# Weight-stationary products in a fused three-block kernel: the two passes of each k-tile one behind the other, instead of eight of the one kind and then eight of the other

## The chip, the cores and the metric

The kernel runs on one core of a Trainium2 chip. The metric is the device time of one execution in microseconds (us); several executions are timed and the median is given. One further execution is recorded instruction by instruction, and every duration below comes from that record. TensorE does the matrix products, VectorE and ScalarE the elementwise work; GpSimd does next to nothing here, and SyncE issues the transfers of the weights.

## The reference

Three transformer blocks run one after the other over 256 tokens of width 1024, all in float32. Blocks 0 and 1 are alike and have their own weights; block 2 has another mixer. What is computed, cut to its shape:

```python
# blocks 0 and 1
h = rms_norm(x, g_pre_mix)
q, k, v, cb, cc, cx, ga, gb = split(h @ w_in)          # 1024 x 6656
y_attn = band_attention(rope(q), rope(k), v, sink) @ w_attn_proj
y_conv = (cb * short_conv(cc * cx, conv_w)) @ w_conv_proj
x = x + rms_norm((sigmoid(ga) * y_attn + sigmoid(gb) * y_conv) @ w_out, g_post_mix)
h = rms_norm(x, g_pre_ffn)
x = x + rms_norm((silu(h @ w_gate) * (h @ w_up)) @ w_down, g_post_ffn)   # inner width 2816
# block 2: a condition vector c gives shifts, scales and gates (silu(c) @ w_cond + b_cond);
# its mixer is a stick-breaking attention beside a trailing mean; its feed-forward part is as above
```

All weights are read from HBM once per execution.

## The kernel before

**Two-part products.** TensorE takes a reduced float32 form here (`F32R`). To keep the accuracy, the kernel splits an operand into a high part H, a copy rounded to that form, and a low part L, the rest. A product of an activation x and a weight w is made of three parts, xH·wH, xL·wH and xH·wL; the fourth is left out. ScalarE writes H of the weights (line 278), VectorE writes L (line 280).

**The weight stream.** The weights are packed in pieces of 128 x 2048 in the order of use (`ORDER`). SyncE loads each as two halves of 128 x 1024 into seven buffers (`emit_raw`, line 258); `emit_half` splits each half into H and L, with twelve buffers for each of them. `get(key)` hands out the next piece, and sees to it that pieces some places further on are loaded and split.

**Two kinds of products.** In the token-major kind (`mmA4`, `mmD2`) the activations are the stationary operand and 512 columns of weights stream past them; each k-tile costs two matmuls of 512 columns with wH and one of 512 with wL. In the weight-stationary kind, `mmB` (line 439), a 128 x 128 tile of weights is loaded into the array and the activations of all 256 tokens stream past. The pair (xH, xL) lies side by side (`xp.hl(k)`), so that one matmul of 512 columns does xH·wH and xL·wH, into the two halves of one PSUM tile `o`; a matmul of 256 columns adds xH·wL to the first half (`xp.k(0, k)` is xH). For one output block of 128 columns there are eight k-tiles. `mmB` does two such blocks (`for c in range(2)`), each made of eight matmuls of 512 columns with H, then eight of 256 with L, and `use(c, o)` then adds the two halves of `o` on ScalarE and VectorE (`both`, lines 456 to 458). In what follows, these sixteen matmuls are called a group, and the matmuls the H pass and the L pass of a k-tile. Every matmul has a weight load of its own in front of it.

`mmB` is used for `cc`, `cx`, `cb` of blocks 0 and 1 (line 882 onwards; PSUM tiles `pcc`, `pcx`, `pcb`), and for nine of the pieces of gate and up in each of the three feed-forward parts (lines 568 and 572; tiles `pg`, `pu`). Block 2's mixer does not use it.

**The order around it.** The program order on TensorE is fixed while the kernel is built. A virtual clock (`clock`, advanced by `pe(ns)` after each matmul with a nominal duration) says when waiting tasks are due: a generator handed to `spawn` runs up to its next `yield`, and names there the delay after which it goes on. `tick()` runs whatever is due, so a task's matmuls land only where a `tick()` stands. In `mmB` it stands behind the fourth H pass, behind the eighth, and at the end of the group. The tasks that land in `mmB` are the attention of blocks 0 and 1 (`keys` and eight `unit`s, lines 614 to 706, spaced by `UNIT` = 10 virtual us; a unit transposes q, computes scores `S`, waits `SM_DELAY` = 8 virtual us for the softmax on VectorE and ScalarE, transposes the probabilities into `PTp`, and multiplies by v), and the transposes `ptf` of the feed-forward part (line 541).

Of the kernel before, what the change touches and what calls it, by code (L numbers as in the profile page):

```python
# [21 lines left out]
KT = D // P  # L22
# [140 lines left out]
def tile_model(ctx: ExitStack, tc: tile.TileContext, x_in, wpack, sink, convw, gains, c_in,  # L163
# [15 lines left out]
    def ps1(name, shape=(P, 512), dt=F32):  # L179
        return pp.tile(list(shape), dt, tag="B", name=name, bufs=8)  # L180
# [41 lines left out]
    def pe(ns):  # L222
        clock[0] += ns / 1000.0

    def tick(limit=None):
        limit = clock[0] if limit is None else limit
        while True:
            due = [e for e in tasks if e[0] <= limit]
            if not due:
                return  # L230
            e = min(due, key=lambda v: v[0])
            tasks.remove(e)
            d = next(e[1], None)
            if d is not None:
                tasks.append([max(e[0], clock[0]) + d, e[1]])
# [10 lines left out]
    def mm(o, a, b, start, stop, **kw):  # L246
        nc.tensor.matmul(o, a, b, start=start, stop=stop, **kw)  # L247
# [191 lines left out]
    def mmB(name, w, xp, use):  # L439

        for c in range(2):
            o = ps1(f"{name}_{c}", (P, 2, T))
            H, L = (v.rearrange("p (k c) -> p k c", k=KT) for v in w[c])
            for k in range(KT):
                mm(o, H[:, k, :], xp.hl(k), k == 0, False)
                pe(213)
                if k == 3:
                    tick()
            tick()
            for k in range(KT):  # L450
                mm(o[:, 0], L[:, k, :], xp.k(0, k), False, k == KT - 1)
                pe(107)
            use(c, o)
            tick()

# [78 lines left out]
    def ffn(l, xp, norms, make_post, after, early=lambda: None):  # L534
# [29 lines left out]
        for key in order:  # L564
            cond_due()
            if key[0] == "g":
                s = s2(f"s{l}{key[2]}", (P, 2, T))
                mmB(f"pg{l}{key[2]}", get(key), xp, lambda c, o: both(s[:, c], o))
                last = nc.scalar.activation(s, s, AF.Silu)  # L569
            elif key[0] == "u":  # L570
                fv = s2(f"f{l}{key[2]}", (P, 2, T))
                mmB(f"pu{l}{key[2]}", get(key), xp, lambda c, o: both(fv[:, c], o))
                nc.vector.tensor_mul(fv, fv, s)  # L573
                fHL = s4(f"fHL{l}{key[2]}", (P, 2, 2, T), F32R)
                nc.scalar.copy(fHL[:, 0], fv)  # L575
                nc.vector.tensor_sub(fHL[:, 1], fv, fHL[:, 0].bitcast(F32))
                fs.append((fHL[:, 0], fHL[:, 1]))
            else:
                j = key[2]
                if not accs:  # L580
                    drain()
                    accs = [[ps1(f"dn{l}_{t}{c}") for c in range(2)] for t in range(2)]
                if j == NDOWN - TAIL - 2:
                    early()
                if j < NDOWN - TAIL:
                    w = get(key)
                    for t in range(2):
                        for c in range(2):
                            mmD2(accs[t], w, fs[j][0], fs[j][1], t, c, j == 0, False)
                else:  # L590
                    cap = 2 * (state["use"] - len(tail)) + NSPLIT
                    tail.append((get(key, cap), fs[j][0], fs[j][1]))
# [260 lines left out]
    def mixer1(l, xp, norms):  # L853
# [28 lines left out]
        for j in range(4):  # L882
            cc = s2(f"cc{l}{j}", (P, 2, T))
            mmB(f"pcc{l}{j}", get(("cc", l, j)), xp, lambda c, o: both(cc[:, c], o))
            u = ac.tile([P, 2, T + 2], F32, tag="u", name=f"u{l}{j}", bufs=1)
            nc.vector.memset(u[:, :, 0:1], 0.0)
            nc.vector.memset(u[:, :, T + 1:T + 2], 0.0)
            mmB(f"pcx{l}{j}", get(("cx", l, j)), xp, lambda c, o: both(u[:, c, 1:T + 1], o))
            nc.vector.tensor_mul(u[:, :, 1:T + 1], u[:, :, 1:T + 1], cc)
            y = s2(f"yc{l}{j}", (P, 2, T))  # L890
            for c in range(2):
                w = cw[:, l, 2 * j + c, :]
                nc.vector.tensor_scalar(y[:, c], u[:, c, 0:T], w[:, 0:1], None, ALU.mult)
                nc.vector.scalar_tensor_tensor(y[:, c], u[:, c, 1:T + 1], w[:, 1:2], y[:, c], ALU.mult, ALU.add)
                nc.vector.scalar_tensor_tensor(y[:, c], u[:, c, 2:T + 2], w[:, 2:3], y[:, c], ALU.mult, ALU.add)
            b = s2(f"cb{l}{j}", (P, 2, T))
            mmB(f"pcb{l}{j}", get(("cb", l, j)), xp, lambda c, o: both(b[:, c], o))
            nc.vector.tensor_mul(y, b, y)
            yp.put(2 * j, 2, y)
# [161 lines left out]
    xp = Pair("x0")  # L1061
    norms = None

    for l in range(DEPTH):
        mp = mixer1(l, xp, norms)
        gpm, gpf = row(4 * l + 1, f"gpm{l}"), row(4 * l + 2, f"gpf{l}")
        xp = Pair(f"xf{l}")
# [38 lines left out]
        xp, norms = nxp, nn  # L1106
# [23 lines left out]
    xp = Pair("xf2")  # L1130
# [95 lines left out]
```

## Time and profile before

| | |
|---|---|
| times of three executions | 1142.68, 1144.66, 1146.54 us |
| their median | 1144.66 us |
| the profiled execution: its own time | 1144.54 us |
| its span, first to last instruction | 1142.4 us |
| VectorE busy | 800.3 us (70%) |
| ScalarE busy | 687.2 us (60%) |
| transfers of weights | 422, of 512 KB, median 5.1 us from issue to landing |
| HBM read | 233.28 MB |
| mean granted TensorE clock | 0.998 |

How to read it: a matmul's busy time in such a record runs from its start to its modelled end, and consecutive matmuls overlap, so the busy time of TensorE says that it had something in flight, not what a matmul costs. What a matmul costs in a row of them is the distance between the starts of two neighbours, called a step below.

### The profile page before, as it was taken

The page shows a single profiled execution, that of the slowest core. Times are in us where ns is not written, and L with a number is a line of the kernel's source. Part 1 is how long each engine was busy: PE and PEld are TensorE (multiplying, and loading weights), DVE is VectorE, ACT ScalarE, POOL GpSimd, SP SyncE. Part 2 cuts the span into 40 slices and gives each one's busy share as a digit, 9 for nine tenths or more (in the row PEclk, how much of TensorE's full clock was granted, in tenths as well). Part 3 has the DMA queues.
Part 4 walks back from the last instruction along what each step waited for, and adds up shares of the span by engine and source line. Part 5 has one row for each costly group of instructions (what it writes and reads, how often), then busy time and mean ns, then how long its engine had stood idle before and what let it go on. Part 6 is the DMA issues. An engine that isn't in the chain of part 4 may idle for free.

```text
span 1142.4 us, 15967 instructions
## 1 busy us (share of the span) xinstructions
PE 1132.2 (99%) x5901; PEld 951.7 (83%) x5901; DVE 800.3 (70%) x1188; ACT 687.2 (60%) x1209; POOL 13.4 (1%) x28
## 2 busy tenths in 40 slices
PE   8999999999999999999999999999999999999997
PEld 5888878888888888888878888888888778888886
DVE  7888745658977657798874758977657748866652
ACT  6778766547555446688765556545445847655441
POOL 0000000000000000000000000000000000000000
PEclk9999999999999999999999999999999999999999
DMA  7944346537987752835686538987773653855610
GB/s 286 367 131 160 118 148 210 187 137 253 351 286 244 248 203 85 303 129 166 203 269 211 178 118 275 354 275 243 254 265 104 228 167 110 312 185 185 200 58 37
DMA packets 67039, 235.39 MB, mean 206 GB/s; under 512 B 8849, under 2 KB 9361, under 8 KB 66962
## 3 DMA queue, kind: packets, MB, share of 16 engines
q1 hardware_dynamic: 63216, 224.83, 57.3%
q10 hardware_dynamic: 3746, 9.56, 2.5%
q8 instruction: 46, 0.75, 0.3%
q14 instruction: 31, 0.25, 0.1%
HBM read 233.28 MB, written 1.07 MB: 205 GB/s over the span
## 4 chain that ended last, share of the span: by engine, by line
PE 95%; DMA 2%; DVE 1%; issue 1%; ACT 0%; DVEq 0%; POOLq 0%; POOL 0%; ACTq 0%; SPq 0%
PE dn L247 15%; PE pu L247 14%; PE pg L247 13%; PE wo L247 5%; PE pcc L247 4%; PE pap L247 4%; PE pgb L247 4%; PE pga L247 4%; PE pcx L247 4%; PE pcp L247 4%; PE pcb L247 3%; PE pq L247 3%; PE puA L247 3%; PE pgA L247 3%; PE pkv L247 2%; PE po L247 1%
## 5 line engine op out<-in xcount | busy, mean ns | idle before, releaser
L280 DVE TENSOR_TENSOR L<-raw,H 128x1024 fp32r<-128x1024 f32 x370 | 445.4, 1220 | 141.1 <-ACT H L278 131.5
L278 ACT CAST H<-raw 128x1024 fp32r<-128x1024 f32 x370 | 383.5, 1052 | 153.8 <-issue 40.8
L247 PE MATMUL dn<-H,fHL 128*128 128x512 f32 x432 | 116.1, 390 | 0.0
L247 PE MATMUL pu<-xf,H 128*128 128x512 f32 x432 | 108.2, 392 | 0.0
L247 PE MATMUL pg<-xf,H 128*128 128x512 f32 x432 | 107.8, 391 | 0.0
L247 PEld LDWEIGHTS dn<-H,fHL 128*128 128x128 f32 x432 | 79.8, 188 | 15.6
L247 PEld LDWEIGHTS pg<-xf,H 128*128 128x128 f32 x432 | 79.2, 188 | 15.2
L247 PEld LDWEIGHTS pu<-xf,H 128*128 128x128 f32 x432 | 77.7, 189 | 13.9
L528 DVE SCALAR_TENSOR_TENSOR raw<-raw,silu_c 128x1024 f32<-128x1024 f32 x48 | 58.4, 1219 | 27.0 <-DMA raw<-in_wpack_dram 26.9
L247 PE MATMUL dn<-L,fHL 128*128 128x512 f32 x216 | 66.6, 389 | 0.0
L247 PEld LDWEIGHTS pg<-xf,L 128*128 128x128 f32 x432 | 58.9, 190 | 4.2
L247 PEld LDWEIGHTS pu<-xf,L 128*128 128x128 f32 x432 | 58.9, 190 | 4.2
L247 PE MATMUL pu<-xf,L 128*128 128x256 f32 x432 | 60.2, 282 | 0.0
L247 PE MATMUL pg<-xf,L 128*128 128x256 f32 x432 | 60.2, 282 | 0.0
L247 PE MATMUL wo<-H,m 128*128 128x512 f32 x192 | 52.9, 396 | 0.1
L575 ACT CAST fHL<-f 128x512 fp32r<-128x512 f32 x27 | 16.7, 620 | 54.1 <-DVE f L573 54.1
L247 PEld LDWEIGHTS dn<-L,fHL 128*128 128x128 f32 x216 | 40.5, 188 | 8.6
L569 ACT ACTIVATE s<-s 128x512 f32<-128x512 f32 x27 | 17.1, 632 | 43.4 <-DVE s L458 43.3
L247 PEld LDWEIGHTS wo<-H,m 128*128 128x128 f32 x192 | 35.4, 188 | 8.1 <-DVE m L212 0.6
L247 PE MATMUL pap<-H,o 128*128 128x512 f32 x128 | 35.2, 394 | 0.0
L247 PE MATMUL pcp<-H,y 128*128 128x512 f32 x128 | 35.1, 395 | 0.0
L670 ACT ACTIVATE P<-S,nm 128x256 f32<-128x256 f32 x64 | 29.5, 478 | 3.5 <-DVE nm L664 3.5
(290 smaller groups left out, 1927.6 us busy)
## 6 DMA issues: line engine op xcount, KB each, us to landing
raw<-in_wpack_dram SPq DMA_DIRECT2D x422, 512.0 KB, 5.1
gpm<-in_gains_dram ACTq DMA_DIRECT2D x3, 512.0 KB, 7.9
gpf<-in_gains_dram ACTq DMA_DIRECT2D x3, 512.0 KB, 8.9
gqf<-in_gains_dram ACTq DMA_DIRECT2D x2, 512.0 KB, 6.5
out_dram<-x SPq DMA_DIRECT2D x4, 256.0 KB, 2.0
pmat<-in_pmat_dram SPq DMA_DIRECT2D x2, 384.0 KB, 7.4
x<-in_x_dram SPq DMA_DIRECT2D x2, 256.0 KB, 3.0
x<-in_x_dram SPq DMA_DIRECT2D x1, 512.0 KB, 7.0
```

The lines of the kernel that those rows point to most:

```text
L247: nc.tensor.matmul(o, a, b, start=start, stop=stop, **kw)
L278: nc.scalar.copy(H, r)
L280: nc.vector.tensor_sub(L, r, H.bitcast(F32))
L528: nc.vector.scalar_tensor_tensor(w[u], w[u], 1.0, silu_c, ALU.mult, ALU.mult, accum_out=mcol[:, r, 2 * j + u:2 * j + u + 1])
L569: last = nc.scalar.activation(s, s, AF.Silu)
L575: nc.scalar.copy(fHL[:, 0], fv)
L670: nc.scalar.activation(Pt[:, hh, :], S[hh // 2][:, hh % 2, :], AF.Exp, bias=nm[:, hh:hh + 1], accum_out=den[:, hh:hh + 1])
```

## The change

Inside `mmB`, each k-tile's L pass now follows its H pass directly. Both belong to one accumulation into the same PSUM tile; the two matmuls that close it are those of the last k-tile. The nominal durations of 213 and 107 ns become one of 340 ns for the pair, and the inner `tick()`s stand behind the third and the sixth pair, with the last one where it was.

```diff
             for k in range(KT):
-                mm(o, H[:, k, :], xp.hl(k), k == 0, False)
-                pe(213)
-                if k == 3:
+                mm(o, H[:, k, :], xp.hl(k), k == 0, k == KT - 1, skip_group_check=True)
+                mm(o[:, 0], L[:, k, :], xp.k(0, k), False, k == KT - 1, skip_group_check=True)
+                pe(340)
+                if k in (2, 5):
                     tick()
-            tick()
-            for k in range(KT):
-                mm(o[:, 0], L[:, k, :], xp.k(0, k), False, k == KT - 1)
-                pe(107)
             use(c, o)
             tick()
```

The number of matmuls, of weight loads and of columns that stream stays as it was, and so does the number of `tick()`s. `skip_group_check` concerns the building of the program alone.

## The prediction

> **What bounds the kernel now.** I began with the page: the span, the engines' busy time, the shares of the chain that ended last. Then I asked what TensorE waited for.
>
> ```profile
> span 1142.4 us, 15967 instructions
> PE 1132.2 (99%) x5901; PEld 951.7 (83%) x5901; DVE 800.3 (70%) x1188; ACT 687.2 (60%) x1209; POOL 13.4 (1%) x28
> ...
> PE 95%; DMA 2%; DVE 1%; issue 1%; ACT 0%; DVEq 0%; POOLq 0%; POOL 0%; ACTq 0%; SPq 0%
> ```
>
> ```profile
> PE warm_ps L247 <- DVE warm L309: 1.5, 1, 1.5
> PE pq L644 <- DVE qs L639: 0.9, 1, 0.9
> PE pq L247 <- DVE Lq L723: 0.8, 1, 0.8
> PE pq L247 <- ACT Hq L718: 0.4, 1, 0.4
> PE pt L752 <- DVE xg L723: 0.2, 1, 0.2
> ```
>
> The second fence is the whole list of waits of TensorE: 3.8 us in 1142.4, of which only the 0.9 us lies beyond the start of the kernel. TensorE is the chain, and the time is the sum of its steps. So I priced the steps, not the busy time. The time of this execution is 1144.54 us, 2.1 over its span and 0.1 under the median of the runs; the sum is made against 1144.54.
>
> **What a step costs today.** The timeline of TensorE over the two blocks of one `pu` piece, its columns being start, length (first start to last end), and count:
>
> ```profile
> 281.24 2.00 PE L247 MATMUL pu<-xf,H 128*128 128x512 f32 x8
> 283.08 1.11 PE L247 MATMUL pu<-xf,L 128*128 128x256 f32 x8
> 284.04 2.00 PE L247 MATMUL pu<-xf,H 128*128 128x512 f32 x8
> 285.88 1.12 PE L247 MATMUL pu<-xf,L 128*128 128x256 f32 x8
> 286.83 0.40 PE L247 MATMUL pg<-xf,H 128*128 128x512 f32 x1
> ```
>
> Eight H passes take 283.08 - 281.24 = 1.84 us, 0.230 a step; eight L passes 284.04 - 283.08 = 0.96, 0.120 a step. The chain of work gives both blocks together, and a long row of nothing but 512-column matmuls in comparison:
>
> ```profile
> 162.28 21.76 PE pgb L247 x96
> ...
> 281.41 5.59 PE pu L247 x32
> ```
>
> A group is 5.59 / 2 = 2.795 us. In the undisturbed row a 512-column step is 21.76 / 96 = 0.2267 us, so eight H passes could take 1.813 instead of 1.84: about 0.027 us is lost behind each row of L passes. Narrow windows show where. First the H passes, in single rows:
>
> ```profile
> 281.24 0.40 PE L247 MATMUL pu<-xf,H 128*128 128x512 f32 x1
> 281.71 0.39 PE L247 MATMUL pu<-xf,H 128*128 128x512 f32 x1
> ```
>
> Two steps take 0.47, 0.235 each: H passes are slow right behind a row of L passes and come back to 0.2267 later. And the L passes (each row starts with the next one):
>
> ```profile
> 285.88 0.40 PE L247 MATMUL pu<-xf,L 128*128 128x256 f32 x2
> 285.99 0.40 PE L247 MATMUL pu<-xf,L 128*128 128x256 f32 x2
> 286.11 0.40 PE L247 MATMUL pu<-xf,L 128*128 128x256 f32 x2
> 286.23 0.40 PE L247 MATMUL pu<-xf,L 128*128 128x256 f32 x2
> ```
>
> The first L pass, the one that follows an H pass, takes 0.11 us, the next ones 0.12. Half of 0.2267 is 0.1133: the first L pass runs at the same rate per column as the undisturbed H passes, and the others 0.0067 slower. My reading is that TensorE needs about 0.12 us from one weight load and matmul to the next; a long H pass leaves time to prepare the next pair, a row of short ones uses that lead up after one step, and the following H passes need several steps to win it back.
>
> **The change, part by part.** *The steps.* In the new order each L pass stands behind an H pass. A pair of 0.2267 + 0.1133 = 0.340 us has a mean step of 0.170, above the 0.12 at which short ones run dry. If every L pass is then like the first one (0.1133) and every H pass like the undisturbed one (0.2267), a group takes 8 x 0.340 = 2.720 us, 0.075 less than 2.795. The upper end for a pair is that no pass recovers, 0.235 + 0.120 = 0.355, 2.840 a group. The two middle ends, H alone or L alone at its better value, stand among the rivals. I take 0.340, because the two better values are the ones that the trace shows with the neighbours that each pass will have (an L pass behind an H pass) or with the lead that a mean step of 0.170 should leave.
>
> How many groups: the L passes, eight to a group.
>
> ```profile
> L247 PE MATMUL pu<-xf,L 128*128 128x256 f32 x432 | 60.2, 282 | 0.0
> L247 PE MATMUL pg<-xf,L 128*128 128x256 f32 x432 | 60.2, 282 | 0.0
> ...
> L247 PE MATMUL pcx<-x,L 128*128 128x256 f32 x64 | 9.4, 284 | 0.0
> L247 PE MATMUL pcb<-x,L 128*128 128x256 f32 x64 | 9.2, 284 | 0.0
> L247 PE MATMUL pcx<-xm,L 128*128 128x256 f32 x64 | 9.1, 283 | 0.0
> L247 PE MATMUL pcb<-xm,L 128*128 128x256 f32 x64 | 9.1, 284 | 0.0
> L247 PE MATMUL pcc<-x,L 128*128 128x256 f32 x64 | 9.0, 284 | 0.0
> L247 PE MATMUL pcc<-xm,L 128*128 128x256 f32 x64 | 9.0, 284 | 0.0
> ```
>
> That is 2 x 432 + 6 x 64 = 1248 matmuls, 156 groups; 156 x 0.075 = **11.7 us less**. The `dn` products behind a `pu` group lose the 0.027 too, at most 27 times, 0.7 us; I leave it out of the sum and put it into the lower end.
>
> *The operands.* L of the first k-tile is needed 0.23 us after the group's start instead of 1.84, and H is held to the end, 2.72 instead of 1.84. What hides both is the ring of split weights:
>
> ```profile
> ACT H L278 <- PE pg L247: 19.0, 16, 1.2
> ```
>
> ScalarE waits for TensorE to give back buffers of H, so in the feed-forward parts the splits fill all twelve; and the waits of TensorE above hold no line for an L from line 280. Cost taken: nothing. If the cover were gone, the price would be up to 1.6 us a group. Buffers given back 0.9 us later delay only transfers and splits that are several pieces ahead; VectorE, the busier of the two, has room even in the stretch with the attention and in the first feed-forward part (columns: window, length, then busy time on PE, PEld, DVE, ACT):
>
> ```profile
> 48.00:135.00 87.00, 87.00 (x568) 76.57 (x567) 74.77 (x171) 72.19 (x177) 0.00 (x0) 1.00 0.45 157
> ...
> 276.00:415.00 139.00, 139.00 (x750) 120.39 (x749) 107.02 (x144) 75.69 (x108) 0.00 (x0) 1.00 0.82 285
> ```
>
> *The virtual clock and the ticks.* A group was 8 x 320 = 2.56 virtual us and took 2.795; it becomes 2.72 and takes 2.72. So a delay of 8 virtual us of a softmax shrinks from 8 x 2.795 / 2.56 = 8.73 to 8.0 us, 0.73 less, while VectorE and ScalarE need as long as before. Behind a transpose that comes too early, all of TensorE's queue stands. There are places with no room today:
>
> ```profile
> 494.56 1.71 ACT L677 ACTIVATE P<-P,rd 128x256 f32<-128x256 f32 x4
> ...
> 496.37 0.82 PE L685 MATMUL PTp<-ident,P 128*128 128x128 f32 x6
> ```
>
> P is ready at 496.27 and its transposes start 0.10 later. Sixteen units (eight in each of two blocks) of 0.73 make 11.7 us at the very most; the lower end is that the one wait there is now goes, -0.9. I take **1.0 us more**, the value nearest to the only wait of this kind on the list (0.9): the three ticks of a group are about 0.9 us apart, so most dues are rounded up by more than what they lose, and TensorE itself has no other late start on its list.
>
> *Sum:* 1144.5 - 11.7 + 1.0 = **1133.8 us**, about 0.9% less.
>
> **The rivals.** (1) *Half of it: L wins, H does not.* If H passes keep the mean of today's block, 0.230, since each has an L pass in front of it, a pair is 0.3433, a group 2.747, and the time 1144.5 - 156 x 0.048 + 1.0 = 1138.0. For it: an H pass behind L passes is the slow one today. Against it: it is slow behind eight of them, and no row shows it behind a single one.
>
> (2) *The order is indifferent.* Each step would belong to the matmul that streams, whoever its neighbours are: there are as many loads under H passes and as many under L passes as before. If only the disturbance of the H passes goes (0.2267 + 0.120), a group is 2.773, 3.4 us less in all, 1142.1; if nothing goes, 1145.5. For it: the 0.12 is very regular. Against it: the first L pass's 0.11. The Trainium skill, TensorE: Matmul & The Clock Gate, "What happens when you issue a matmul", speaks for this rival: the weight load is pulled ahead into a background buffer, and does not take read bandwidth from the running matmul, so that each load hides under whatever streams. Its "Back-to-back issue gap" gives N / 2.4 + 2.5 ns, by which an estimate of a pair is 325 ns in either order; the trace has 0.2267 us for 512 columns where that gives 0.216, so these figures do not hold here, and I use none of them.
>
> (3) *Slower.* If the lead, once used up by an L pass, is not won back in the one H pass that follows, every H pass is like the first two behind a row of L passes, 0.235, and every L pass like the later ones, 0.120: 2.840 a group, 156 x 0.045 = 7.0 us more, 1152.5 with the 1.0. It decides as soon as a pair takes over 0.349. For it: today the H passes need several steps to recover, not one. Against it: one H pass alone leaves 0.1 us more than the 0.12 that I think a pair needs to be made ready.
>
> **How the numbers follow.** Forecast 0.52, rival 1 0.16, rival 2 0.20, rival 3 0.10, something else, such as the units' waits at several us on top of the gain, 0.02. A measurement here can tell about 0.3%, 3.4 us, from no change. Faster by more: the forecast, rival 1 and the rest, 0.70; within it: rival 2, 0.20; slower: rival 3, 0.10. The range: low, 1144.5 - 11.7 - 0.9 - 0.7, 1131; high, to 1143, which takes in rival 1, the waits of the units at a few us, and the better half of rival 2; left out are its other half and rival 3, 2 in 10.
>
> **What would show it.** In the profile after, a `pu` or `pg` piece of 32 matmuls should take 5.44 us in the chain instead of 5.59 (rival 1: 5.49; rival 2: 5.55 to 5.59; rival 3: 5.68), and the steps from H to L and from L to H should be 0.227 and 0.113. The list of TensorE's waits should have no line for an L of line 280, and at most some 2 us on `PTp`, `S` and `pq`. The prediction is wrong if a piece is not at 5.44, or if it is and waits in the attention have taken the gain.

## The result, and the profile after

| | before | after |
|---|---|---|
| median of the runs | 1144.76 us | 1154.72 us |
| ratio, 95% interval | | 1.0089, 1.0077 to 1.0101 |
| the profiled execution: its own time | 1144.54 us | 1155.41 us |
| its span | 1142.4 us | 1153.2 us |

The change makes the kernel 0.9% slower; 1133.8 us had been predicted. From the page of the changed kernel, busy time and the chain:

```profile
span 1153.2 us, 15964 instructions
PE 1139.8 (99%) x5901; PEld 950.9 (82%) x5901; DVE 800.8 (69%) x1188; ACT 687.2 (60%) x1209; POOL 13.5 (1%) x28
...
PE 90%; DVE 3%; DMA 2%; ACT 2%; issue 2%; DVEq 0%; POOLq 0%; POOL 0%; ACTq 0%; SPq 0%
```

As many matmuls and loads as before, and the same work on the other engines; TensorE is still nearly the whole chain, but ScalarE and VectorE now hold some of it. (The busy time of the weight loads fell by 0.8 us while the span rose by 10.8; it says nothing of this change.) To see where the time went, I cut both chains of work at products that the change leaves alone. Their starts, before:

```profile
35.57 10.88 PE pkv L247 x48
...
437.15 8.22 PE pq L247 x36
...
459.89 10.88 PE pkv L247 x48
...
588.06 21.76 PE pgb L247 x96
...
893.24 7.05 PE pv L247 x30
...
1114.37 15.36 PE dn L247 x68
```

and after:

```profile
35.97 10.88 PE pkv L247 x48
...
164.70 21.76 PE pgb L247 x96
...
441.38 8.19 PE pq L247 x36
...
464.11 10.88 PE pkv L247 x48
...
595.47 21.76 PE pgb L247 x96
...
902.50 7.05 PE pv L247 x30
...
1125.18 15.40 PE dn L247 x68
```

| stretch | before | after | more |
|---|---|---|---|
| `pkv` to `pgb`, block 0: `cc`, `cx`, `cb`, with the attention | 126.71 | 128.73 | 2.0 |
| `pgb` to `pq`: holds the first feed-forward part | 274.87 | 276.68 | 1.8 |
| `pkv` to `pgb`, block 1 | 128.17 | 131.36 | 3.2 |
| `pgb` to `pv`: the second feed-forward part | 305.18 | 307.03 | 1.9 |
| `pv` to the last `dn` products: block 2, the third | 221.13 | 222.68 | 1.6 |

Half of the 10.4 us between these cuts is in the two mixers, half in the three feed-forward parts. In the feed-forward parts the pieces have become longer. Before, from the chain:

```profile
386.70 5.56 PE pg L247 x32
392.26 5.59 PE pu L247 x32
397.85 5.47 PE dn L247 x24
```

After, one round early in the first feed-forward part and a later one:

```profile
290.03 5.55 PE pg L247 x32
295.58 5.55 PE pu L247 x32
301.12 5.47 PE dn L247 x24
...
390.56 5.64 PE pg L247 x32
396.20 5.65 PE pu L247 x32
401.85 5.50 PE dn L247 x24
```

A usual round is 0.08 + 0.06 + 0.03 = 0.17 us longer. The first rounds of the parts change less than that; added up over all gate, up and `dn` products of the three parts, the longer steps make some 3.8 us, and the other 1.4 are steps held up ahead of the transposes `ptf`, below. The forecast had been 5.44 for a piece. The early round is the same code, and shorter: pieces of 5.55, 0.347 us a pair, and later ones of 5.65, 0.353. (The first round of the second part runs at 5.55 too, that of the third at 5.65.) The single steps at the head of a later gate piece, which begins behind a row of 512-column matmuls, from the timeline:

```profile
306.43 0.39 PE L247 MATMUL pg<-xf,H 128*128 128x512 f32 x1
306.66 0.28 PE L247 MATMUL pg<-xf,L 128*128 128x256 f32 x1
306.77 0.40 PE L247 MATMUL pg<-xf,H 128*128 128x512 f32 x1
307.00 0.28 PE L247 MATMUL pg<-xf,L 128*128 128x256 f32 x1
307.12 0.40 PE L247 MATMUL pg<-xf,H 128*128 128x512 f32 x1
307.36 0.28 PE L247 MATMUL pg<-xf,L 128*128 128x256 f32 x1
307.48 0.40 PE L247 MATMUL pg<-xf,H 128*128 128x512 f32 x1
307.72 0.28 PE L247 MATMUL pg<-xf,L 128*128 128x256 f32 x1
```

The first pair takes 306.77 - 306.43 = 0.34 us, as forecast for all of them. From its L pass on, L passes take 0.11, 0.12, 0.12 and H passes 0.23, 0.24, 0.24: 307.72 - 306.66 = 1.06 us for three pairs, 0.353 each, and then the pattern begins again. After the first one, no H pass has the 0.2267 of an undisturbed row. There are new waits too, most of them in the mixers; the head of the list of TensorE's waits after the change:

```profile
PE PTp L682 <- ACT P L674: 1.8, 2, 1.1
...
PE pq L641 <- DVE qs L636: 1.2, 2, 0.8
PE ptf L541 <- DVE sA L556: 1.0, 2, 0.6
```

`PTp`, the transposes of the probabilities, and `ptf` were not on it before. The view of line 682 says how long its engine sat idle before it, and until what (time, times):

```profile
  ACT P L674: 6.0, 11
```

This adds the idle time of the weight loads (4.3 us) to that of the matmuls (1.8), which overlap, and neither is what TensorE lost. That comes from the distances between starts, and is an estimate: the steps ahead of the `PTp` matmuls are some 4.2 us longer in all than usual steps of the same kind, those ahead of `ptf` 1.5 and those ahead of `pq` 1.6. Before the change the three were 0.05, 0.1 and 1.2.

### The profile page after: what moved, and what is told of

It reads as the page before. It is cut to its first block, busy times and chain, and to the rows that moved or that the text cites. A ratio compares the mean times of both kernels' runs of the same rounds, so it can differ in the third digit from the quotient of the medians.

```text
span 1153.2 us, 15964 instructions
## 1 busy us (share of the span) xinstructions
PE 1139.8 (99%) x5901; PEld 950.9 (82%) x5901; DVE 800.8 (69%) x1188; ACT 687.2 (60%) x1209; POOL 13.5 (1%) x28
## 4 chain that ended last, share of the span: by engine, by line
PE 90%; DVE 3%; DMA 2%; ACT 2%; issue 2%; DVEq 0%; POOLq 0%; POOL 0%; ACTq 0%; SPq 0%
PE dn L247 15%; PE pu L247 14%; PE pg L247 13%; PE wo L247 5%; PE pcp L247 4%; PE pap L247 4%; PE pgb L247 4%; PE pga L247 4%; PE pcx L247 3%; PE pq L247 3%; PE pcb L247 3%; PE pcc L247 2%; PE pgA L247 2%; PE pkv L247 2%; PE puA L247 2%; DMA raw<-in_wpack_dram 2%
## 5 line engine op out<-in xcount | busy, mean ns | idle before, releaser
L247 PE MATMUL pg<-xf,H 128*128 128x512 f32 x432 | 153.6, 398 | 0.0
L247 PE MATMUL pu<-xf,H 128*128 128x512 f32 x432 | 153.4, 398 | 0.0
L247 PE MATMUL pu<-xf,L 128*128 128x256 f32 x432 | 121.1, 280 | 0.0
L247 PE MATMUL pg<-xf,L 128*128 128x256 f32 x432 | 121.1, 280 | 0.0
L247 PEld LDWEIGHTS pu<-xf,H 128*128 128x128 f32 x432 | 81.1, 188 | 20.0
L247 PEld LDWEIGHTS pg<-xf,L 128*128 128x128 f32 x432 | 81.5, 189 | 0.9
L247 PEld LDWEIGHTS pu<-xf,L 128*128 128x128 f32 x432 | 81.5, 189 | 0.0
L455 DVE TENSOR_TENSOR f<-pu,f 128x256 f32<-128x256 f32 x54 | 22.6, 418 | 17.3 <-ACT f L454 17.3
```

The costliest lines, as they stand in the source:

```text
L455: nc.vector.tensor_add(dst, o[:, 0], dst)
```

## The experiments

Theory A was: two causes, the steps of the pairs and the faster virtual clock. The first two kernels separate them.

**Pairs, old clock.**

```diff
-                pe(340)
+                pe(320)
```

> The pairs as in the changed kernel, but the nominal duration of a pair back at 320 ns, so that the virtual clock runs as before the change; the ticks stay behind the third and sixth pair. Theory A (two causes: the steps of the pairs themselves, about 5 us over the three feed-forward parts and 1.5 us over the two mixers; and the faster virtual clock, which makes the attention's tasks come too early, about 3.5 us): feed-forward parts as in the changed kernel, mixers 3 to 4 us shorter than there, 1151 us in all. Rival B (the clock is innocent, the places of the ticks between the pairs cost the mixers their time): 1155 us, as the changed kernel.

Measured 1150.77 us, 1.0057 of before (1.0042 to 1.0072). The feed-forward parts keep their loss: a gate and an up piece run from 337.37 to 348.66, 5.65 each.

```profile
337.37 0.39 PE L247 MATMUL pg<-xf,H 128*128 128x512 f32 x1
...
348.66 1.11 PE L247 MATMUL dn<-H,fHL 128*128 128x512 f32 x4
```

The mixers are 1.1 and 0.7 us longer than before (`pkv` at 34.48 and 461.30, `pgb` at 162.32 and 590.16), not 2.0 and 3.2. Theory A holds, B falls. The old clock does not take every new wait away: the view of line 682 still has 2.1 us, in 4 places, so the pairs, or the places of their `tick()`s, bring some of them alone.

**Old order, new clock.** Eight and eight as before, with the nominal durations changed.

```diff
-                pe(213)
+                pe(227)
...
-                pe(107)
+                pe(113)
```

> Eight H passes and then eight L passes as before, but nominal durations of 227 and 113 ns, 2.72 us for a group, as in the changed kernel. Theory A (steps and clock both cost): feed-forward parts as before apart from up to 1 us of waits at the transposes behind the first pieces, mixers 3 to 4 us longer, 1148 us. Rival B (clock innocent): 1144.8 us, as before.

Measured 1145.84 us, 1.0013 (1.0004 to 1.0023). The feed-forward parts are as before, the mixers 0.1 and 1.0 us longer. So the clock alone costs 1 to 1.5 us, not the 3 to 4 expected: it hurts mainly together with the pairs. The softmax is waited for here too (the view of `PTp`, line 685 in this kernel, has 3.3 us in 5 places), but the old wait of 0.9 us of `pq` is no longer on the list.

**What of the clock?** The changed kernel with one constant raised.

```diff
-SM_DELAY = 8.0
+SM_DELAY = 8.75
```

> The changed kernel with its nominal 340 ns, and the softmax delay raised from 8 to 8.75 virtual us, which in real time is what 8 was before the change; all else as changed. Theory M (the transposes of the probabilities that come too early are what the faster virtual clock costs): the waits of PTp in the mixers go, 2 to 2.5 us less than the changed kernel, 1152.4 us. Rival N (the whole attention is pressed together, so what is spared at the probabilities is waited for at the next transposes of q or the scores): within 1 us of the changed kernel, 1154 to 1155.

Measured 1150.15 us, 1.0054 (1.0037 to 1.0071): 0.35% below the changed kernel's ratio, some 4 us, nearly twice what was expected. The view of the same line 682 now reads

```profile
  ACT P L674: 0.2, 1
```

and the mixers are 0.7 and 0.2 us longer than before (`pkv` at 35.20 and 461.83, `pgb` at 162.65 and 590.25). The two mixers together are 4.2 us shorter than in the changed kernel, and by the distances between starts the steps ahead of `PTp` account for 3.9 of it. The waits for the softmax are thus most of what the faster clock costs: M holds in kind, N falls. `pq` still waits 1.6 us here. (At the measured 2.82 us a group this delay is 8.75 x 2.82 / 2.72 = 9.07 real us, a little more than the 8.73 of before, by estimate.)

**Is a lead used up and won back?** This was the prediction's reading. One L pass is put among the H passes:

```diff
-            8 x H, then 8 x L
+            H0 L0 H1 H2 H3 H4 H5 H6 H7 L1 L2 L3 L4 L5 L6 L7
```

> Order H0 L0 H1 ... H7 L1 ... L7, nominal durations and number of ticks as before the change: one single L pass stands among the H passes. Theory A (one short matmul puts the H passes behind it out of step just as a row of eight does, and they need five or so to come back): the steps of H1 to H5 read about 233, 236, 228, 232, 231 ns. Rival E, the reading of the prediction (an L pass uses up only as much lead as it is short of, so that one H pass wins it back): H1 at 227 to 230, the rest at 227.

The timeline of a group behind a long row of `dn` products:

```profile
337.52 0.39 PE L247 MATMUL pg<-xf,H 128*128 128x512 f32 x1
337.75 0.28 PE L247 MATMUL pg<-xf,L 128*128 128x256 f32 x1
337.86 1.77 PE L247 MATMUL pg<-xf,H 128*128 128x512 f32 x7
339.48 0.76 PE L247 MATMUL pg<-xf,L 128*128 128x256 f32 x5
```

The single L pass takes 0.11, as forecast. But the seven H passes behind it take 339.48 - 337.86 = 1.62 us, 0.231 each, instead of 7 x 0.2267 = 1.587. Step by step they read 232, 236, 228, 233, 231, 226, 227 ns, which is 0.026 us too much: as large a loss behind one L pass as it was behind a row of eight (0.027). The reading of the prediction (E) falls: the gain of the L pass is given back, several times over, by the H passes behind it. In the groups that follow, the single L pass falls among H passes that are out of step already, and seven are not enough to come back: 241, 237, 234, 235, 225, 230, 236 ns in one of them. The pieces take 5.59 and 5.61 us, against 5.56 and 5.59 before; the kernel was timed once, at 1146.10 us.

**Other orders.** Three more, the rows of four timed once:

```diff
+            turned pairs:  H L L H  H L L H  H L L H  H L L H
+            rows of two:   H H L L  H H L L  H H L L  H H L L
+            rows of four:  H H H H  L L L L  H H H H  L L L L
```

> Order H L L H H L L H in each group: as many H and L passes as before, every second pair turned round, so that half of the H passes stand behind an H pass and half of the L passes behind an L pass; ticks behind six and twelve matmuls; nominal durations 227 and 113. Theory A (an H pass is slow as long as the last few matmuls in front of it held a short one, 0.233 to 0.236 us, an L pass costs 0.113 behind an H pass and 0.119 behind an L pass): 0.35 us for an H and an L together, 2.80 a group, feed-forward parts about 2 us longer than before. Rival C (it is the number of changes from one length to the other that costs, sixteen in a group of the changed kernel, two before, eight here): halfway between before and the changed kernel in the feed-forward parts, 2.5 us longer than before. Rival D (order indifferent once the rows of L passes are broken up): 0.347 a pair, 2.77 a group, 3 us shorter than before in the feed-forward parts.

> Order H H L L in each group, nominal durations as before the change, ticks behind six and twelve matmuls. Theory F (a pair of passes costs 0.2267 + 0.120 = 0.3467 us in any order, 2.773 a group, since a short pass that gets away with 0.1133 hands the difference to the next H pass; on top of it some orders run into a repeating pattern that loses about 0.02 us each time round): a group between 2.773 and 2.822 us; the time between 1142 and 1150, with 1145 the likeliest, since half of the matmuls have a neighbour of their own length as in the turned pairs (2.786). Rival A (an H pass is slow as long as a short one was among the last few): 0.35 a pair, 2.80 a group, 1146. The prediction's own reading, that a lead is used up and won back: 0.340 to 0.345 a pair, 2.72 to 2.76, 1138 to 1141.

> Order H H H H L L L L, twice in a group, nominal durations as before the change. Theory F: 2.773 and one loss of 0.02 us behind each of the two rows of L passes, 2.81 a group, if four H passes are not enough to fall back into step, or two losses of less. Rival A: the same four slow H passes behind each row of L passes, 233 + 236 + 228 + 232 ns, and 113 + 119 + 120 + 120 for the L passes, 2.80 a group. Told apart by the single steps, not by the sum: under F they need not repeat from row to row.

| order | changes of length in a group | gate and up piece together | a pair | ratio to before |
|---|---|---|---|---|
| rows of eight (before) | 2 | 5.56 + 5.59 | 0.348 | 1 |
| rows of four | 4 | 5.58 + 5.61 | 0.350 | one run, 1145.79 us |
| turned pairs | 8 | 342.96 - 337.39, twice | 0.348 | 1.0013 (1.0003 to 1.0022) |
| rows of two | 8 | 5.56 + 5.57 | 0.348 | 1.0005 (0.9995 to 1.0015) |
| pairs | 16 | 5.64 + 5.65 | 0.353 | 1.0089 (1.0077 to 1.0101) |

The pieces of three of them, from the chain (rows of four, rows of two) and the timeline (turned pairs, starts of a gate piece, an up piece and what follows):

```profile
404.06 5.58 PE pg L247 x32
409.65 5.61 PE pu L247 x32
```

```profile
403.85 5.56 PE pg L247 x32
409.41 5.57 PE pu L247 x32
```

```profile
337.39 0.39 PE L247 MATMUL pg<-xf,H 128*128 128x512 f32 x1
...
342.96 0.39 PE L247 MATMUL pu<-xf,H 128*128 128x512 f32 x1
...
348.53 1.07 PE L247 MATMUL dn<-H,fHL 128*128 128x512 f32 x4
```

The number of changes does not set the cost (C falls: eight changes are no dearer than two), and A's sizes, 0.35 for the turned pairs and the rows of two, are a little high for both. D's 0.347 is near, but its gain of 3 us did not come. Laid end to end, the turned pairs are rows of two shifted by one pass, so these two kernels are nearly one test. Their single H passes read 230 to 236 ns (227 right behind a `dn` row), the L passes 112 to 120. F's sum fits best: the rows of two came out at 2.78 us a group and 1145.37 us, where the prediction's own reading had 1138 to 1141. In the rows of four the H steps differ from one row to the next (235, 233, 236, 224 and then 233, 236, 228, 233 ns), which F allows and A does not. All orders lie between 0.347 and 0.353 a pair, and none comes near 0.340. No order beats the kernel before beyond the measurement.

**Does the start of a row choose its pattern?** In the changed kernel the pairs run at 0.347 in the first round of the first and the second feed-forward part, where they begin behind float32 transposes (`ptf`). The third part begins behind such transposes too and runs at 0.353, which speaks against the theory from the start. Here a transpose stands ahead of each gate piece.

```diff
+            if name[:2] == "pg" and c == 0:
+                nc.tensor.transpose(o[:, 0, 0:P], ident, ident)
```

> The pairs with nominal durations of 320 ns, and one float32 transpose of 128 columns ahead of each gate piece's first group; its result is overwritten. Theory F, second part (the pattern that a row of pairs falls into depends only on how it starts: behind a row of 512-column matmuls into the one of 0.353 us a pair, behind a float32 transpose into the one of 0.347): all gate and up groups of the feed-forward parts at 2.773 us, pieces of two groups at 5.55 instead of 5.65; the transposes themselves cost about 0.2 us each, 27 of them, so that the time is within 2 us of the kernel without them. Rival G (the better pattern behind the first transposes has to do with the place in the feed-forward part, such as fewer transfers or splits beside it): pieces at 5.65 wherever they are at 5.65 without the transposes.

Timed once, at 1152.59 us, it is 1.8 above the pairs without the transposes, but its pieces are not the shorter ones; they take 5.64 and 5.66:

```profile
406.93 5.64 PE pg L247 x32
412.57 5.66 PE pu L247 x32
```

Theory F's second part falls: a transpose ahead of a row does not choose the better pattern. It can change the pattern, and either way: around the one ahead of the second gate piece the `pu` pieces go from 5.55 to 5.65 in the first feed-forward part, and from 5.66 to 5.55 in the third. What chooses is open.

**Which difference upsets the steps?** The H and L passes differ in the weight tile and in length. Three kernels, each timed once, keep the pairs (clock at 320) and lengthen the L pass, to 512, 384 and 288 columns.

```diff
-                mm(o[:, 0], L[:, k, :], xp.k(0, k), False, ...)
+                mm(o, L[:, k, :], xp.hl(k), False, ...)          # 512; 384 and 288: the first columns of both
```

> The pairs, but the L pass also streams 512 columns, xH and xL, so that the fourth part xL wL is added too; nominal durations of 320 ns for the pair. Theory F (the short pass is what upsets the steps; weight loads that alternate between the tiles of H and of L do no harm): every step 0.2267 us, 16 x 0.2267 = 3.627 a group, 7.25 a piece. Rival H (it is the changing between the two weight tiles, or two matmuls running into the same half of one PSUM tile, that slows the H passes): steps of 0.231 to 0.241 among them, 3.70 or more a group.

> The pairs with nominal durations of 320 ns, the L pass streaming 384 columns instead of 256: xH and the first 128 tokens of xL, so that the fourth part is added for these tokens. Theory J (a weight load that runs beside a pass needs about 0.12 us; a pass of 256 columns, 0.1133, is 0.0067 too short to hide it, and either it or the H pass behind it pays, in any order; a pass of 384 columns, 0.170, hides it): steps of 0.227 and 0.170 throughout, 3.173 us a group, 6.35 a piece. Rival K (passes of two lengths in turn upset each other, however long): H passes at 0.231 to 0.241, 3.21 or more a group.

> As before, with 288 columns in the L pass (0.1275 us at the rate of 512 columns in 0.2267): xH and the first 32 tokens of xL. Theory J: 0.1275 is just over 0.12, steps of 0.227 and 0.1275 throughout, 2.833 a group and 5.67 a piece, no more than 0.02 over the 5.65 of the pairs with 256 columns, although an eighth more columns stream in the L passes. Rival L (the load needs more than 0.1275 beside a pass, and the loss shrinks with the length but is not gone): H passes still at 0.230 to 0.236 and a group of 2.85 to 2.89.

With 512 columns, from the chain, every step is the undisturbed one: 7.25 / 32 = 0.2266.

```profile
417.79 7.25 PE pu L247 x32
```

So the change of weight tile and the common PSUM tile do no harm (F's part on this holds, H falls). With 384 columns the disturbance is back, though 0.170 us is well over 0.12:

```profile
344.47 0.34 PE L247 MATMUL pu<-xf,L 128*128 128x384 f32 x1
344.64 0.39 PE L247 MATMUL pu<-xf,H 128*128 128x512 f32 x1
344.87 0.34 PE L247 MATMUL pu<-xf,L 128*128 128x384 f32 x1
345.05 0.40 PE L247 MATMUL pu<-xf,H 128*128 128x512 f32 x1
```

H passes 0.23, L passes 0.17 to 0.18; a piece of 32 takes 6.50 or 6.51, 0.406 a pair, where the rates of an undisturbed row make 0.2267 + 0.170 = 0.3967 (in the first rounds of the parts 6.61, 0.413). With 288 columns a piece takes 5.81, 0.363, where they make 0.354. From the chains of the two, 384 columns first:

```profile
344.40 6.51 PE pu L247 x32
```

```profile
346.66 5.81 PE pu L247 x32
```

J falls, and with it the reason that F gave, a short pass that costs 0.12 us; rival L falls too, since the loss does not shrink with the length. K stands: passes of two lengths in turn lose 0.009 to 0.010 us a pair, whether the short one has 288 or 384 columns (0.016 in the first rounds with 384), and 0.007 or 0.013 with 256. The columns of PSUM that a pass writes changed along with its length, so which of the two matters is not shown. The Trainium skill, TensorE: Matmul & The Clock Gate, "What happens when you issue a matmul", has weight loads pulled ahead, so that the next tile's weights load while the present matmul runs. The row with equal lengths agrees; the rows with 288 and 384 columns show a loss that this rule does not explain, since the load has more time there than under 256 columns.

## Why the prediction was wrong

- *What bounds the kernel*: right. TensorE's steps are the time, before and after, and 156 groups lengthened by hundredths of a microsecond show in the total.
- *The steps*, the term of 11.7 us less: this is where it failed. It joined the best L pass (0.1133) and the best H pass (0.2267) of the old order, with the reason that a mean step of 0.170 leaves the lead that a short pass needs, so that the one H pass between two L passes recovers; its own reading of the old order had been that H passes need several steps for that. Both values were read rightly, but they have different neighbours: 0.2267 belongs to an H pass with no short pass among the five or more ahead of it. In the pairs there is always one, and only the first pair behind an undisturbed row takes 0.340. The kernel with one L pass among H passes shows it directly: behind an undisturbed row, one short pass slows the H passes behind it as much as a row of eight. A pair measured 0.353 (on average H 0.237, L 0.117), close to the 0.355 of rival 3, which had 0.10. That the H pass does not recover in the one step that it has is what the runs show; the reason, a lead that steps under 0.12 use up, is not, since beside passes of 384 columns the H passes are slow too. Instead of 11.7 less the steps brought some 3.8 us more in the feed-forward parts and, by what the waits leave over, some 0.7 in the mixers. (A smaller slip: 2.795 is a group of an up piece; a gate piece took 5.56, 2.78 a group.)
- *The evidence was there.* The prediction priced the loss behind a row of L passes at 0.027 us, about four times the 0.0067 that a first L pass saves. It treated the 0.027 as a cost of the row, paid once in eight pairs and so to be removed; the run with one L pass shows it as a cost of having just had a short pass.
- *The virtual clock and the ticks*, 1.0 us more: right in kind, too small. The mechanism was named (a softmax delay 0.73 us shorter, transposes that come too early) and the run with a delay of 8.75 brings the idle time ahead of `PTp` from 6.0 to 0.2 us in the view, and from 4.2 to 0.3 by the distances between starts. Of the 10.4 us, some 5.9 are such waits, where 1.0 was taken: about 4.1 ahead of `PTp`, 1.4 ahead of `ptf`, which the prediction did not name, and 0.4 ahead of `pq`. The bound of 11.7 held; the list of waits in the old profile was a poor guide, since it shows what waits, not what has no room.
- *The operands*: right; no wait for an L from line 280 appeared.
- *Rivals*: rival 1 and the forecast needed an L pass that keeps 0.1133, which one in three does, and rival 2 the indifference of the order. In a loose sense rival 2 was near: all orders tried cost 0.347 to 0.353 a pair, and its 0.3467 is what the luckier pattern of the changed kernel shows (5.55 a piece). That is a coincidence of the sum, for the H passes are disturbed in this pattern too, 231 to 233 ns.
- *The range*, 1131 to 1143, left out the slower rival. It gave no weight to the fact that the two losses, steps and waits, have separate causes and add up. Rival 3's 1152.5 came nearest, but partly by luck: it had 7.0 us of steps, where some 4.5 came, and 1.0 of waits, where some 5.9 came.

What stays open: why passes of two lengths in turn lose these nanoseconds, why the loss has two sizes in the same code (0.347 and 0.353 a pair), and why the faster clock, which makes `PTp` wait in both orders, costs 1 to 1.5 us in the old order and some 4 with the pairs.

## What to carry to other kernels

A step time read from a trace belongs to the neighbours that it had: before adding the best values of two kinds of step, look for a place where both occur side by side in the new order, and if there is none, take the disturbed values as the likelier ones. On an engine that is 99% busy, an order that mixes long and short matmuls closely is no gain as such; here keeping equal lengths together, in rows of two or of eight, was as good as anything. Where a program order is made by a virtual clock, its nominal durations are part of the schedule: changing them moves every delay, and those delays that just cover another engine's work turn into waits.

## What the hardware showed unexpectedly

- Steps of matmuls repeat to a nanosecond or so and depend on more than the matmul just ahead: behind a short pass that follows an undisturbed row, the 512-column passes read 232, 236, 228, 233, 231 ns before they are back at 227; behind one that follows a disturbed row, seven are not enough.
- Mixed lengths cost more than the sum of their own rates: 0.353 against 0.340 us for 512 + 256 columns, 0.406 (0.413 in the first rounds) against 0.397 for 512 + 384, 0.363 against 0.354 for 512 + 288; 512 + 512 costs nothing extra, with two weight tiles in turn.
- The same row of pairs can settle into two patterns, 0.347 and 0.353 us a pair, and keeps the one that it is in for whole pieces; one transpose between two pieces was seen to change it either way.
